# Modulation vectors added up on VectorE over two layers, and expert gathers planned with a longer landing

## The chip, the core and the metric

The kernel runs on one NeuronCore of a Trainium2 chip. Five engines with queues of their own work side by side: TensorE (matmuls and transposes; PE in the rows), VectorE (DVE), ScalarE (ACT), GpSimd (POOL) and SyncE (SP), which here issues the plain loads and stores. GpSimd issues the indirect ones. Each engine works through its queue strictly in order, and an instruction that waits holds up all behind it. The metric is device time in microseconds (us), the lower the better.

## The reference

Two blocks over 512 tokens of width 1024, in float32. The first block has two layers, each with three mixers: a gated delta rule, latent attention and a gated linear recurrence. The second block takes modulation vectors from two conditioning vectors `c` and `c_ctx`, runs differential attention and retention over 512 tokens and 256 context tokens, and then a mixture of 64 experts.

```python
mod_x = jax.nn.silu(c) @ ada_w[l] + ada_b[l]
mod_c = (jax.nn.silu(c_ctx) @ ada_w[l] + ada_b[l])[None]
...
sh1, sc1, g1, sh2, sc2, g2 = jnp.split(mod_x, 6, axis=-1)
csh1, csc1, cg1, csh2, csc2, cg2 = jnp.split(mod_c, 6, axis=-1)
...
x = x + g1[:, None] * y_x
h2 = modulate(rmsnorm_2(x, norm2_g), sh2, sc2)
ffn_x = moe_ffn(h2.reshape(b * s, d), router_w, router_bias, exp_w1, exp_w3, exp_w2,
                shared_w1, shared_w3, shared_w2).reshape(b, s, d)
x = x + g2[:, None] * ffn_x
...
def body(acc, inp):                       # in moe_ffn, over blocks of one expert's tokens
    tok, wt, e = inp
    xb = h_pad[tok]
    yb = (jax.nn.silu(xb @ w1[e]) * (xb @ w3[e])) @ w2[e]
    return acc.at[tok].add((yb * wt[:, None].astype(yb.dtype)).astype(acc.dtype)), None
```

`ada_w` is 1024 x 6144, and of `mod_c` only the first two of six parts are used. Each token goes to 8 of the 64 experts. The modulation vectors depend on the conditioning vectors alone, not on `x`, so they can be computed at any time before the second block.

## The kernel before

The kernel is written as a recording. Every engine call goes into a list (`Rec.add`), with its reads and writes, and at `flush` a list scheduler (`Rec.attempt`) replays the list on a model of the engines and so decides the order in which each engine's instructions are written. All instructions but a few thus have one source line (L411 before, L415 after). The model takes a duration from `cost` for each instruction, a latency from `lat` between dependent ones (2000 ns behind any DMA), and `move` (bytes over 360 per ns) for the transfer. A free engine takes the ready instruction with the highest priority, which is the longest path to the end plus a bias. An instruction with a `gate` is not ready before a given earlier instruction has started.

Tiles come from pools of fixed buffers. `s2`, `wh` and `wl` are 80 buffers of 128x512 (`b` in the rows); `wr` and `ad` are three and four of 128x1024 (`raw`). A matmul of full precision is done as three fp32r matmuls on a high and a low half of each operand; `split` makes the halves, the high one on ScalarE and the low one, a subtraction, on VectorE (`b<-raw,b`). Every weight goes through this, so each engine stands in the path of TensorE's weights.

The first block's layers run as merged generators: `merge` draws from the delta rule, the dense projections and, as a side stream, from `ada`, each in proportion to a weight. `ada` loads the modulation weights in 48 chunks of 128x1024 (six parts of eight), multiplies each chunk by a column of the conditioning vectors on ScalarE (for two vectors in the parts 0 and 1, for one in the others, 64 products) and adds up the products on GpSimd. The delta rule ends its preparation by writing its triangular blocks out (`mdiag`) and reading their diagonals back, with which `gdn_solve` begins.

The routed experts run one after the other (`expert`, `block`), each with a fixed number of slots (`CAPS`, 32 to 192). A block compares slots with positions, selects with four small matmuls against `aux` which token sits in each slot, reduces that on VectorE to a row index `ix`, gathers these rows of `h2d` into X by an indirect DMA from GpSimd, transposes X on TensorE (eight 128xc transposes `ps<-const,raw`), and runs the expert: 4 fp32 and 12 fp32r matmuls, an activation, two transposes, 12 fp32r matmuls. The result Y is scattered with addition into `accd`. An unused slot has an index beyond the tokens: the gather leaves it out, and the scatter sends it to one of 128 spare rows behind the 512. The gather's chain can't start before the instruction that `hold` names, `XAHEAD` marks back, with three marks for each expert; weight loads have their own marks (`RAHEAD`, nine).

## Time and profile before

| quantity | value |
|---|---|
| runs, us | 2386.49, 2395.57, 2395.74 (median 2395.57) |
| profiled execution, us | 2396.73, its span 2395.0 |
| TensorE busy | 2187.3 us, 91% |
| VectorE, ScalarE, GpSimd busy | 1619.6, 1087.7 and 534.6 us |
| mean granted TensorE clock | 0.947 of full speed |
| HBM read and written | 358.44 and 41.63 MB |

The stages by time: first layer to about 605 us, second layer to 1120, second block's projections, attention, retention and routing to 1600, routed experts to 2370, final norm. A row of busy times by stage has the stage, its length, then busy us and instruction count of TensorE, its weight loads (PEld), VectorE, ScalarE and GpSimd, then the granted clock, the DMA engines' mean busy share and GB/s. A row of waits has who waited, for whom, us in total, times and the longest. A row of grouped instructions has engine, operation, written and read tiles with shapes and count, then busy us and mean ns of one, then the engine's idle us before them and what ended it. A row of a timeline has start, duration, engine, operation, and in brackets the idle time before it and its releaser. A row of the chain has start, length, and what was worked on.

### The profile page before, as it was taken

How to read it: one execution, taken by the hardware profiler on the slowest of the kernel's cores; microseconds unless marked ns; L12 is line 12 of the kernel's file. 1: busy time of each engine (PE TensorE's matmuls, PEld its weight loads, DVE VectorE, ACT ScalarE, POOL GpSimd, SP SyncE). 2: the span in 40 equal slices, each digit the busy share in tenths (PEclk: the TensorE clock that was granted, in tenths of full speed). 3: DMA queues.
4: the chain of work that ended last, by engine and by line, in shares of the span. 5: the costliest groups of instructions: out<-in, count | busy, mean ns of one | idle time of the engine just before them, and what ended most of it. 6: DMA issues, size and time to landing. Idle time of an engine off the chain costs nothing.

```text
span 2395.0 us, 32613 instructions
## 1 busy us (share of the span) xinstructions
PE 2187.3 (91%) x10382; PEld 1546.5 (65%) x10382; DVE 1619.6 (68%) x3578; ACT 1087.7 (45%) x2272; POOL 534.6 (22%) x393
## 2 busy tenths in 40 slices
PE   6898988999999999999998879879998999999995
PEld 4677866677788877777886657656555555444442
DVE  7995577775695557767733675657676667776775
ACT  5555456453452365445432353335444444544443
POOL 3364334200021010001000132033232233222222
PEclk9998999899999999999998979989999999999998
DMA  5334354223222232314211025349999899999994
GB/s 191 119 102 127 118 172 146 86 84 124 94 78 74 78 116 75 92 63 143 71 54 53 23 66 198 132 116 348 288 341 282 267 294 313 340 334 302 307 311 130
DMA packets 191185, 398.13 MB, mean 166 GB/s; under 512 B 32169, under 2 KB 48297, under 8 KB 191010
## 3 DMA queue, kind: packets, MB, share of 16 engines
q1 hardware_dynamic: 178050, 356.24, 44.1%
q0 software_dynamic: 12960, 39.79, 7.6%
q8 instruction: 82, 1.34, 0.2%
q14 instruction: 93, 0.76, 0.1%
HBM read 358.44 MB, written 41.63 MB: 167 GB/s over the span
## 4 chain that ended last, share of the span: by engine, by line
PE 69%; DVE 13%; DMA 11%; ACT 3%; issue 3%; POOL 1%; SPq 0%; POOLq 0%; DVEq 0%; ACTq 0%
PE ps L411 69%; DVE b L411 10%; DMA raw<-h2d,m 5%; DVE m L411 3%; ACT b L411 3%; DMA accd<-raw,m 1%; DMA raw<-in_adaw_dram 1%; DMA raw<-in_wo_dram 1%; DMA b<-in_ew_dram 1%; POOL raw L411 1%; DMA xdiag<-b 0%; DMA raw<-in_wi_dram 0%; SPq L411 0%; DMA raw<-accd 0%; DMA b<-in_x_dram 0%
## 5 line engine op out<-in xcount | busy, mean ns | idle before, releaser
L411 PE MATMUL ps<-b,b 128*128 128x512 f32 (+9 forms) x8052 | 1870.1, 389 | 83.2 <-DVE b L411 49.6
L411 PEld LDWEIGHTS ps<-b,b 128*128 128x128 f32 (+6 forms) x8052 | 1312.6, 184 | 571.9 <-issue 130.1
L411 ACT ACTIVATE b<-ps 128x512 f32<-128x512 f32 (+16 forms) x661 | 271.1, 431 | 676.6 <-PE ps L411 599.6
L411 DVE TENSOR_TENSOR b<-b,b 128x512 fp32r<-128x512 f32 (+5 forms) x751 | 469.8, 664 | 35.2 <-ACT b L411 18.3
L411 ACT ACTIVATE b<-b 128x512 fp32r<-128x512 f32 (+3 forms) x702 | 393.8, 619 | 121.6 <-DVE b L411 84.5
L411 DVE TENSOR_TENSOR b<-raw,b 128x512 fp32r<-128x512 f32 (+2 forms) x340 | 240.0, 720 | 187.2 <-ACT b L411 173.7
L411 ACT ACTIVATE b<-raw 128x512 fp32r<-128x512 f32 (+3 forms) x348 | 207.2, 611 | 350.3 <-PE ps L411 256.0
L411 POOL DMA_INDIRECT accd<-raw,m x72 | 133.2, 1850 | 367.6 <-DVE raw L411 224.3
L411 PE MATMUL ps<-const,b 128*128 128x128 f32 (+5 forms) x898 | 159.5, 292 | 52.1 <-DVE b L411 39.0
L411 PEld LDWEIGHTS ps<-const,b 128*128 128x128 f32 (+5 forms) x898 | 115.0, 153 | 102.0 <-DVE b L411 49.4
L411 POOL TENSOR_TENSOR raw<-raw,raw 128x1024 f32<-128x1024 f32 x56 | 140.2, 2512 | 159.9 <-ACT raw L411 132.3
L411 PE MATMUL ps<-raw,b 128*96 128x512 f32 (+5 forms) x272 | 151.8, 676 | 5.3 <-ACT raw L411 2.9
L411 POOL DMA_INDIRECT raw<-h2d,m x68 | 100.9, 1483 | 231.0 <-PE ps L411 83.7
L411 DVE SCALAR_TENSOR_TENSOR raw<-ps,m,b 96x512 f32<-96x512 f32 (+5 forms) x136 | 97.5, 740 | 50.9 <-DMA accd<-raw,m 30.1
L411 DVE SCALAR_TENSOR_TENSOR b<-b,ps 128x512 f32<-128x512 f32 (+6 forms) x106 | 54.1, 510 | 102.7 <-ACT b L411 99.2
L411 POOL TENSOR_TENSOR m<-m,mhalf 128x1 f32<-128x1 f32 (+2 forms) x54 | 52.2, 968 | 301.6 <-DVE m L411 301.6
L411 DVE TENSOR_REDUCE m<-ps 128x1 f32<-128x256 f32 (+9 forms) x196 | 75.1, 393 | 60.5 <-PE ps L411 59.0
L411 DVE TENSOR_TENSOR b<-b,ps 128x512 f32<-128x512 f32 (+6 forms) x150 | 82.6, 559 | 49.2 <-PE ps L411 48.5
L411 DVE TENSOR_TENSOR b<-ps,b 128x512 fp32r<-128x512 f32 (+8 forms) x136 | 74.0, 545 | 47.1 <-ACT b L411 38.9
L411 POOL MEMSET b<- 64x512 f32 (+4 forms) x19 | 8.4, 454 | 398.1 <-PE ps L411 326.6
L411 DVE SCALAR_TENSOR_TENSOR b<-ps,cols,b 128x511 f32<-128x511 f32 (+3 forms) x118 | 86.9, 742 | 7.8 <-ACT b L411 6.9
L411 PE MATMUL ps<-const,raw 96*128 96x96 f32 (+5 forms) x544 | 61.0, 249 | 33.4 <-DMA raw<-h2d,m 30.4
(139 smaller groups left out, 1199.0 us busy)
## 6 DMA issues: line engine op xcount, KB each, us to landing
b<-in_ew_dram SPq DMA_DIRECT2D x640, 256.0 KB
raw<-in_wi_dram SPq DMA_DIRECT2D x100, 512.0 KB
raw<-in_ew_dram SPq DMA_DIRECT2D x64, 512.0 KB
raw<-in_adaw_dram SPq DMA_DIRECT2D x48, 512.0 KB
raw<-in_wo_dram SPq DMA_DIRECT2D x40, 512.0 KB
raw<-in_wuq_dram SPq DMA_DIRECT2D x24, 192.0 KB
b<-in_x_dram SPq DMA_DIRECT2D x16, 256.0 KB
zd<-b SPq DMA_DIRECT2D x16, 256.0 KB
```

The costliest lines, as they stand in the source:

```text
L411: getattr(getattr(nc, o.eng), o.fn)(*[real(x) for x in o.a], **{m: real(x) for m, x in o.k.items()})
```

## The change

In `ada` a chunk's product and addition become one VectorE instruction (`scalar_tensor_tensor`: chunk times column plus sum); only the first product of each sum stays on ScalarE. The side stream is drawn in four slices of 14 steps, one in each half of both layers, at low weights, and a gate keeps each of its instructions from being planned earlier than 60 recorded instructions before it. In the planner an indirect DMA costs 1500 instead of 900 ns of issue, and a gather lands 7000 instead of 2000 ns after its transfer; fp32r matmuls cost 11 ns more and fp32 ones up to 24. The gather's chain may begin nine marks back, three experts, instead of six. A scatter uses the gather's index and leaves out unused slots; the spare rows, their zeros and the second index go.

```diff
+from itertools import islice
...
 RW = 1497.6
 STEP = 4800.0
 AHEAD = 3
-XAHEAD = 6
+XAHEAD = 9
 XBIAS = 6900.0
 NATIVE = 4
-SIDE = ((160, 351), (130, 122))
+SIDE = (11, 12.5)
+SIDEN = 14
 NSLOT = 80
 NADA = 4
 TAGS = {"wl": 5, "wh": 5, "s2": None}
 NRAW = 7
 ADAPS = "tr"
 ADABIAS = 1000000.0
+ADALEAD = 60
 TAIL = 200
+DLAT = (2000.0, 7000.0)
 WIDE = (4, 6)
 LAST = 1
 LASTW = True
...
         if m == "call":
             return 500
         if "dma" in m:
-            return 60 if eng == "sync" else 900
+            return 60 if eng == "sync" else 1500
         n = size(outs[0])
         sb = all("PSUM" not in str(x.space) for x in outs + ins)
         if eng == "tensor":
...
             if dt == BF16:
                 return max(w, 54)
             if dt == F32R:
-                return w + 3 if size(ins[1]) >= 256 else max(4 * w, 108)
-            return max(4 * w, 216)
+                return w + 14 if size(ins[1]) >= 256 else max(4 * w, 108)
+            return max(4 * w + 24, 224)
         if eng == "scalar":
             return 70 + 0.87 * n + (200 if len(outs) > 1 else 50 if len(ins) > 1 else 0)
         if eng == "vector":
...
                 hold.setdefault(o.after, []).append(i)
 
         def lat(p, q):
-            return 2000.0 if "dma" in p.fn else LAT.get(p.eng + q.eng, TAIL)
+            return DLAT[p.k.get("in_offset") is not None] if "dma" in p.fn else LAT.get(p.eng + q.eng, TAIL)
 
         top = {}
         for o in reversed(ops):
...
                     self.issue = max(self.issue, t) + 480
                 self.dmaq = max(self.dmaq, t if e != "sync" else self.issue - 480) + o.move
                 end = self.dmaq
-            done = end + (2000 if "dma" in o.fn else TAIL)
+            done = end + (DLAT[o.k.get("in_offset") is not None] if "dma" in o.fn else TAIL)
             for nm in o.names[1]:
                 self.wrote[nm] = done
             for nm in o.uses:
...
         self.pairs, self.mixB = {}, []
         dense = chain(self.lru(l), self.mla_lat(l), self.mz(l))
         parts = [(self.gdn_chain(l), GW[l]), (dense, 100)]
-        run(merge(*parts, *([(side, SIDE[l][0])] if side else [])))
+        run(merge(*parts, *([(islice(side, SIDEN), SIDE[0])] if side else [])))
         self.load_x()
         self.rope_tables(self.A["const"], 256)
         src = lambda nh, k: self.A["wo"][l, nh, k]
...
                 if h == 3:
                     self.part = list(self.mixB)
 
-        run(merge((heads(), 100), (dense, 60), *([(side, SIDE[l][1])] if side else [])))
+        run(merge((heads(), 100), (dense, 60), *([(islice(side, SIDEN), SIDE[1])] if side else [])))
         run(self.out_proj(src, 4, self.part))
         run(self.out_proj(src, 8, self.mixB[4:8], last=True))
         self.dump_x(f"x{l}")
...
         g = iter(g)
         while True:
             self.nc.bias += ADABIAS
+            self.nc.gate = max(len(self.nc.ops) - ADALEAD, 0)
             try:
                 w = next(g)
             except StopIteration:
                 return
             finally:
                 self.nc.bias -= ADABIAS
+                self.nc.gate = None
             yield w
 
     def ada(self):
...
                     f = sc[:, 8 * v + k:8 * v + k + 1]
                     if not k:
                         nc.scalar.activation(acc[v], w, AF.Copy, scale=f)
-                        continue
-                    pr = w if v == nv - 1 else self.t2(tag="ad")
-                    nc.scalar.activation(pr, w, AF.Copy, scale=f)
-                    nc.gpsimd.tensor_tensor(out=acc[v], in0=acc[v], in1=pr, op=OP.add)
+                    else:
+                        nc.vector.scalar_tensor_tensor(acc[v], w, f, acc[v], op0=OP.mult, op1=OP.add)
                 yield 1.0
             if part < 2:
                 for v in range(nv):
...
 class K3(K2):
     def h2(self):
         nc = self.nc
-        self.acc = self.dr.tile([640, D], F32, name="accd")
+        self.acc = self.dr.tile([T, D], F32, name="accd")
         self.h2d = self.dr.tile([T, D], F32, name="h2d")
         G = [self.mrow(4, i) for i in range(2)]
         S = [self.mrow(3, i) for i in range(2)]
...
                 nr = self.t2()[:, :256]
                 nc.vector.tensor_tensor(out=s3(nr), in0=s3(rem), in1=d, op=OP.subtract)
                 rem = nr
-        self.dump_row = C(1, "dumprow")
-        nc.vector.tensor_scalar(self.dump_row, ipart, 512.0, None, op0=OP.add)
         pc = self.psum("a")
         for t in range(4):
             nc.tensor.matmul(pc[0:64, 0:1], mb[:, 64 * t:64 * t + 64], onesb[:, 0:1], start=(t == 0), stop=(t == 3))
...
         at4 = self.small(4, "at4", I32)
         for t in range(NT):
             nc.vector.tensor_scalar(at4[:, t:t + 1], self.c2[:, 385:386], 128.0 * t, None, op0=OP.add)
-        z = self.t2()
-        nc.gpsimd.memset(z, 0.0)
-        for i in range(2):
-            nc.sync.dma_start(self.acc[512:640, i * 512:(i + 1) * 512], z)
         ph = {(i, j): self.psum("mm") for i in range(2) for j in range(2)}
         at = []
         for h in range(2):
...
             nc.tensor.matmul(pm, oh[:, t, :], aux(t), start=(t == 0), stop=(t == 3))
         m = self.small(2, "m")[:c]
         nc.vector.tensor_reduce(m, pm.rearrange("p (a b) -> p a b", a=2), axis=AX.X, op=OP.add)
-        ix = self.small(2, "ix", I32)[:c]
-        nc.vector.tensor_scalar(ix[:, 0:1], m[:, 0:1], HUGE, None, op0=OP.add)
-        nc.vector.tensor_scalar(ix[:, 1:2], m[:, 0:1], HUGE, self.dump_row[:c], op0=OP.add, op1=OP.min)
+        ix = self.small(1, "ix", I32)[:c]
+        nc.vector.tensor_scalar(ix, m[:, 0:1], HUGE, None, op0=OP.add)
         xs = []
         X = self.t2(tag="wr")[:c]
-        nc.gpsimd.indirect_dma_start(out=X, out_offset=None, in_=self.h2d[:], in_offset=Ind(ix[:, 0:1]),
+        nc.gpsimd.indirect_dma_start(out=X, out_offset=None, in_=self.h2d[:], in_offset=Ind(ix),
                                      bounds_check=T - 1, oob_is_err=False)
         for h in range(2):
             px = self.psum("a")[:, :4 * c]
...
         Y = self.t2(tag=YTAG)[:c]
         for n in range(2):
             nc.vector.scalar_tensor_tensor(Y[:, 512 * n:512 * n + 512], ys[n], m[:, 1:2], self.g2[n][:c], op0=OP.mult, op1=OP.mult)
-        nc.gpsimd.indirect_dma_start(out=self.acc[:], out_offset=Ind(ix[:, 1:2]), in_=Y, in_offset=None, compute_op=OP.add)
+        nc.gpsimd.indirect_dma_start(out=self.acc[:], out_offset=Ind(ix), in_=Y, in_offset=None,
+                                     bounds_check=T - 1, oob_is_err=False, compute_op=OP.add)
 
     def hold(self, q):
         self.nc.gate = self.seen.get(q, self.mark)
```

On TensorE in the expert stage, from one expert's last slot-selection matmul (`aux`) to the transposes of that expert's X (`const,raw` with 128x48), before:

```order
L411 MATMUL ps_70<-aux,b_19467 48x6
L411 MATMUL ps_69<-const_152,b_19542 128x48 x2
L411 MATMUL ps_65<-raw_148,b_19555 48x512 x2
L411 MATMUL ps_65<-b_19203,b_19555 48x512
...
L411 MATMUL ps_67<-b_19538,b_19570 48x512
L411 MATMUL ps_67<-b_19589,b_19570 48x512
L411 MATMUL ps_67<-b_19538,b_19576 48x512
L411 MATMUL ps_71<-const_152,raw_150 128x48 x4
L411 MATMUL ps_72<-const_152,raw_150 128x48 x4
```

and now, at the same place (here the transposes of `raw_150` are those of the expert before, and those of `raw_151` this one's):

```order
L415 MATMUL ps_70<-aux,b_19447 48x6
L415 MATMUL ps_66<-raw_147,b_19559 48x512 x2
...
L415 MATMUL ps_66<-b_19546,b_19566 48x512
L415 MATMUL ps_71<-const_152,raw_150 128x48 x4
L415 MATMUL ps_72<-const_152,raw_150 128x48 x4
...
L415 MATMUL ps_70<-aux,b_19573 48x6
L415 MATMUL ps_65<-raw_146,b_19685 48x512 x2
...
L415 MATMUL ps_65<-b_19672,b_19692 48x512
L415 MATMUL ps_71<-const_152,raw_151 128x48 x4
L415 MATMUL ps_72<-const_152,raw_151 128x48 x4
```

One expert's matmuls stood between selection and transposes; now there are two experts' and one more set of transposes and selections. This holds for 47 of the 68 blocks; for the first few, the last ten and some between the distance is less.

On VectorE in the first layer behind the triangular solve (`b<-ps,m` scales an attention output, `m` are columns, `b<-raw,b` is a weight split), before:

```order
L411 SCALAR_TENSOR_TENSOR b_2336<-b_2327,ps_68 128x512
L411 TENSOR_REDUCE m_10_86<-b_2333 128x4
L411 TENSOR_TENSOR m_10_86<-m_10_86,m_37_113 128x4 x2
L411 TENSOR_SCALAR m_18_94<-m_10_86 128x4
L411 TENSOR_TENSOR b_2363<-raw_151,b_2356 128x512
```

and now:

```order
L415 TENSOR_TENSOR m_26_102<-m_26_102,m_54_130 128x4
L415 SCALAR_TENSOR_TENSOR b_1825<-b_2542,b_1825 128x512
L415 SCALAR_TENSOR_TENSOR raw_147<-raw_145,m_30_106,raw_147 128x1024
L415 SCALAR_TENSOR_TENSOR raw_148<-raw_145,m_30_106,raw_148 128x1024
L415 TENSOR_SCALAR m_3_79<-m_26_102 128x4
L415 TENSOR_TENSOR b_2575<-raw_150,b_2552 128x512
```

The two 128x1024 instructions on `raw` are the new multiply-adds of one chunk for both vectors; the weight split stands behind them. The first pair stands at instruction 362 of VectorE, 36 of the 56 before instruction 820, and the last 20 between 1160 and 1540, in the second layer. On SP's queue the loads of the input `x` are now first; before, two chunks of modulation weights were.

## Rows read from the trace of the kernel before

**Rows 1.** Busy time by stage, columns as above.
```profile
0.00:180.00 180.00, 142.32 (x649) 115.93 (x650) 154.75 (x360) 98.45 (x167) 83.61 (x67) 0.93 0.43 138
180.00:460.00 280.00, 253.88 (x1268) 199.58 (x1267) 180.44 (x308) 146.50 (x251) 103.10 (x49) 0.93 0.42 136
605.00:1120.00 515.00, 502.78 (x2562) 406.61 (x2560) 348.92 (x793) 242.50 (x506) 49.46 (x59) 0.99 0.29 90
1600.00:2340.00 740.00, 696.82 (x2960) 366.30 (x2959) 524.90 (x1130) 345.56 (x747) 220.57 (x132) 0.96 0.97 308
```

**Rows 2.** Waits of TensorE, whole span: us in total, times, longest.
```profile
PE ps L411 <- DVE b L411: 90.0, 63, 10.4
...
PE ps L411 <- DMA raw<-h2d,m: 30.4, 15, 4.7
```

**Rows 3.** Instruction groups of 128x1024 and 1x1024: busy us, mean ns.
```profile
L411 ACT ACTIVATE raw<-raw,m 128x1024 f32<-128x1024 f32 x64 | 73.1, 1144 | 17.1 <-DMA raw<-in_adaw_dram 12.1 <-PE ps L411 4.6 <-DMA modr<-raw 0.3
L411 POOL TENSOR_TENSOR raw<-raw,raw 128x1024 f32<-128x1024 f32 x56 | 140.2, 2512 | 159.9 <-ACT raw L411 132.3 <-DVE b L411 17.3 <-PE ps L411 6.9
L411 DVE SCALAR_TENSOR_TENSOR raw<-raw,raw 1x1024 f32<-1x1024 f32 x1 | 1.2, 1204 | 0.0
```

**Rows 4.** VectorE's groups, 0 to 180 us.
```profile
L411 DVE TENSOR_TENSOR b<-raw,b 128x512 fp32r<-128x512 f32 x39 | 31.5, 817 | 6.0 <-ACT b L411 5.9
...
L411 DVE TENSOR_TENSOR m<-m,m 128x16 f32<-128x16 f32 x11 | 7.7, 697 | 0.2
```

**Rows 5.** VectorE's groups, 180 to 460 us.
```profile
L411 DVE TENSOR_TENSOR b<-raw,b 128x512 fp32r<-128x512 f32 x43 | 38.3, 904 | 32.9 <-ACT b L411 32.9
L411 DVE SCALAR_TENSOR_TENSOR b<-b,b 128x512 f32<-128x512 f32 x16 | 18.9, 1182 | 2.1 <-POOL b L411 1.4 <-ACT b L411 0.5
```

**Rows 6.** VectorE's groups, 605 to 1120 us.
```profile
L411 DVE TENSOR_TENSOR b<-raw,b 128x512 fp32r<-128x512 f32 x112 | 76.1, 694 | 53.9 <-ACT b L411 51.5 <-PE ps L411 2.0
L411 DVE SCALAR_TENSOR_TENSOR b<-b,b 128x512 f32<-128x512 f32 x28 | 19.2, 687 | 8.4 <-ACT b L411 7.4 <-POOL b L411 0.7
...
L411 DVE TENSOR_TENSOR m<-m,m 128x16 f32<-128x16 f32 x11 | 1.8, 167 | 0.0
```

**Rows 7.** The chain that ended last, its start: start us, us, work.
```profile
1.23 4.82 DMA raw<-in_adaw_dram
...
15.01 0.88 DVE b L411 x2
```

**Rows 8.** SP's timeline: the diagonals read, and the second layer's start.
```profile
171.16 0.38 SPq L411 DMA_DIRECT2D b<-mdiag  x1
...
599.71 11.21 SPq L411 DMA_DIRECT2D xd<-b  x5
...
724.69 0.38 SPq L411 DMA_DIRECT2D b<-mdiag  x1
```

**Rows 9.** Waits of ScalarE, 0 to 610 us.
```profile
ACT raw L411 <- DMA raw<-in_adaw_dram: 12.1, 8, 3.1
```

**Rows 10.** TensorE's timeline: a selection and its transposes; two following groups of transposes.
```profile
2064.61 0.29 PE L411 MATMUL ps<-aux,b 128*64 128x6 bf16 x4
...
2079.99 0.71 PE L411 MATMUL ps<-const,raw 64*128 64x64 f32 x8 [1.10 <-DMA raw<-h2d,m]
...
2203.03 0.69 PE L411 MATMUL ps<-const,raw 48*128 48x48 f32 x8
...
2213.34 0.69 PE L411 MATMUL ps<-const,raw 48*128 48x48 f32 x8
```

**Rows 11.** TensorE's waits for gathers: the first, and one near the end.
```profile
1617.97 1.34 PE L411 MATMUL ps<-const,raw 96*128 96x96 f32 x8 [3.53 <-DMA raw<-h2d,m]
...
2312.69 0.43 PE L411 MATMUL ps<-const,raw 32*128 32x32 f32 x4 [1.37 <-DMA raw<-h2d,m]
```

**Rows 12.** Busy time of two stretches of 20 us.
```profile
1680.00:1700.00 20.00, 20.00 (x78) 12.04 (x77) 15.89 (x31) 9.77 (x20) 5.20 (x4) 1.00 1.05 344
...
1800.00:1820.00 20.00, 15.31 (x63) 8.57 (x62) 11.39 (x26) 7.26 (x16) 5.17 (x4) 0.83 0.76 206
```

## The prediction

> **What bounds the kernel now.** I read the busy time by stage first [rows 1]. Two regimes show. From 1600 to 2340 us, the routed experts, TensorE is busy 697 of 740 us and the DMA engines 97%: both are nearly full. From 605 to 1120 us, the second layer of the first block, TensorE is busy 503 of 515 us at a granted clock of 0.99, so TensorE alone bounds it. The first layer does the same work from 0 to 605 us and needs 90 us more: TensorE is idle 38 us of its first 180 and 26 us of the next 280, at a granted clock of 0.93 in both.
>
> Then I read whom TensorE waits for. VectorE is the largest item; in the expert stage the gathers (15 waits, 30.4 us) are the only large one, and expert weights are not in the list at all [rows 2]. So the change can gain in two places: the first layer, and the gather waits with the clock that they cost.
>
> **Modulation vectors.** Before, each of 64 products is a ScalarE pass of 1144 ns, and 56 of them are added on GpSimd at 2512 ns, 140 us in all, within the first layer [rows 3]. After, 8 ScalarE passes stay, the 56 adds go, and VectorE gets 56 fused multiply-adds of 128x1024. The trace has one VectorE instruction of this form, on one partition: 1204 ns [rows 3]. I take that for each: 56 x 1.204 = 67 us of new VectorE work. ScalarE loses 56 x 1.144 = 64 us, GpSimd 140 us.
>
> VectorE also wins something. The same forms are slower while GpSimd adds than in the second layer, where it doesn't [rows 4 to 6]. First 180 us: weight subtractions 39 x (817-694) ns = 4.8 us, 128x16 products 11 x (697-167) = 5.8 us, together 11 us. From 180 to 460 us: 43 x (904-694) = 9.0 us and 16 x (1182-687) = 7.9 us, together 17 us. These are the largest groups only, so the excess is not less than 28 us.
>
> A rule bears on this. The Trainium skill, SBUF — State Buffer, section "SBUF: two separate sides", says that a VectorE instruction with two SBUF inputs and a GpSimd instruction take a port pair as an exclusive lock, the later one waiting out the other. Taken literally an add could hold VectorE for its whole 2.5 us, 140 us in all; the rows of the largest groups show 28 us, and the sum uses the rows. The rule also speaks against the change, since each new multiply-add would hold off GpSimd for 1.2 us, 67 us in all; no row has TensorE waiting for GpSimd.
>
> *Start.* The first two chunks of the modulation weights stand ahead of the input rows on SP's queue and lead the chain for 4.8 us [rows 7]. After, the input rows are first: -4 us (bounds -4.8 and 0).
>
> *Up to the triangular solve.* In the new VectorE order 362 instructions precede the first multiply-add; before, VectorE runs 360 in the first 180 us [rows 1]. So this stage becomes free of modulation work. From its first VectorE work (15.0 us) to the read of the block diagonals (171.2 us) it takes 156 us; the same piece of the second layer, from 599.7 to 724.7 us, takes 125 us [rows 7, 8]. The difference, 31 us, is the most to gain; the largest VectorE groups account for 11. The passes that ScalarE loses and the clock come on top, so I take two thirds of the ceiling: -21 us (bounds -31 and 0).
>
> *Rest of the first layer.* 36 of the 56 multiply-adds now stand here, 43 us of VectorE against at least 17 us of lost excess: 26 us more on an engine with 100 us idle in 280 [rows 1]. That idle time hides it; if the cover fails it costs 26 us, and if TensorE's idle 26 us came back, it would gain those. Between them, with the freed ScalarE: -4 us.
>
> *Second layer.* The other 20, 24 us, go where VectorE is busy 349 of 515 us. Bounds 0 and +24; TensorE is the bound there, so +4 us.
>
> What is queued behind a multiply-add: it waits for its 512 KB chunk, and behind it on VectorE stand the weight splits that TensorE needs. Before, ScalarE stood in this place and waited 12.1 us, in 8 of the 48 chunks [rows 9]. This lies inside the bounds above, and has a rival below.
>
> Layers together: -4 - 21 - 4 + 4 = -25 us.
>
> **Gathers: planned later, issued earlier.** At full clock one expert takes 10.31 us of TensorE, the distance between two groups of input transposes [rows 10]. Before, from an expert's slot-selection matmuls to its transposes there is one period less these two (0.69 and 0.29 us): 9.3 us. In the new order a whole expert more stands between: 19.6 us. Selection, GpSimd's issue and landing have to fit in. A long one: selection at 2064.61, transposes released at 2079.99, so 15.4 us [rows 10]. That overruns 9.3 and fits 19.6. For the first four, the last ten and some seven between, the distance stays near the old one.
>
> So of the 30.4 us the first wait (3.53 us) and those of the last ten experts (1.37 us and a smaller one) stay; 25 us go [rows 2, 11], where one of the seven can still wait. The bounds are 0 and -27.
>
> Stalls also cost clock: in a full stretch it is 1.00, in one with a stall and 15.31 of 20 us busy it is 0.83 [rows 12], a mixture of the 1.2 and 2.4 GHz levels. In the whole stage 0.04 x 740 = 30 us of full-speed work is missing; two thirds of it, -20 us, I put to the waits that go (bounds 0 and -27).
>
> Late next are the weights. The stage moves 740 us x 308 GB/s = 228 MB; at the 344 GB/s of the full stretch [rows 12] that is 663 us, under the some 700 us that would remain. So DMA keeps a cover of about 5%, less than before: +3 us for new waits (bounds 0 and +30, had DMA to stay near its present rate). Padded scatter rows: the capacities add up to 5104 slots for at most 4096 tokens, so some 1000 rows of 4 KB go, 4 MB written and as much read for the accumulation, 12 to 24 us of DMA time by the same rate. TensorE doesn't wait for it, so I count nothing, but it widens the cover. One small VectorE instruction less per block, a zero tile and two stores less: nothing, for VectorE is idle 215 us of this stage.
>
> X lives longer in its buffer, some 20 us of a turn of 31 us with three buffers, so GpSimd gets no new wait there, and the scatters behind it none.
>
> Experts: -25 - 20 + 3 = -42 us.
>
> **New TensorE costs in the planner** (11 ns more for each fp32r matmul, 24 for fp32 ones) reorder everything, the attention stage of the second block too. No row tells the sign: 0, with the spread of the three runs (2386.5 to 2395.7) as bounds, -9 and +9.
>
> **Sum.** -25 - 42 = -67 us. The profiled run took 2396.7 us (span 2395.0, and 1.7 around it), 1.1 us over the median of 2395.6: 2396.7 - 67 - 1.1 = 2328.6, 2328 us. What a measurement here can tell from no change is about 0.5%, 12 us.
>
> **Rivals.**
> 1. *The multiply-adds become TensorE's wait in both layers.* For: TensorE already waits longest for VectorE [rows 2], and in the new order up to ten multiply-adds stand within 28 instructions. Against: 100 and 166 us of VectorE idle in these stages. Price, nothing hidden: -4 - 21 + 26 + 24 = +25, with the experts' -42: -17, 2379 us. Chance 0.13.
> 2. *Weights bound the experts.* For: DMA at 97% [rows 1]. Against: 228 MB fit in 663 us, and TensorE's waits don't name weights. With the +30 in full the experts give -15: -25 - 15 = -40, 2356 us. A milder form is gathers that still land late because the queues are fuller. Chance 0.11.
> 3. *Slower: VectorE stands still for each chunk.* The planner's landing for plain loads is unchanged, 2 us after the transfer, while a chunk leads the chain for 4.8 us at the start [rows 7]; in parts 0 and 1 each chunk goes to the same buffer, so none is loaded ahead. If each of 48 chunks holds VectorE and with it TensorE for 3.1 us, the longest wait of ScalarE before [rows 9], that is +149: with -25 and -42, +82, 2478 us. It decides from 67/48 = 1.4 us for every chunk; before it was 12.1/48 = 0.25 us. Chance 0.07.
>
> The forecast itself has 0.69, with a range of its own from 2290 to 2362: half of both gains gives 2362; the gather and clock bounds (12 more), the ceiling before the solve (10) and three quarters of the idle time behind it (16) give 2290. The whole range adds the reordering on the low side and reaches rival 1 on the high side: 2284 to 2380. It leaves out rival 3 and the tails. Faster by over 0.5% (under 2384 us): the forecast, rival 2 and most of rival 1, 0.88. Within: 0.05. Slower: rival 3, 0.07.
>
> **What would show it.** Right: TensorE's waits for gathers fall from 30 us to under 8 and stay only in the first and last experts; granted clock of the expert stage 0.98 or more, in some 700 us with DMA at 95% or above; weight subtractions near 694 ns in the first 180 us; the diagonals read near 146 us; multiply-adds near 1.2 us, with VectorE waiting for modulation chunks by less than 20 us. Wrong: TensorE waiting for weight splits in the second layer, VectorE waiting for chunks by over 1.4 us each, or an expert stage of 740 us with weights among the waits.

## The result, and the profile after

The changed kernel takes 2356.48 us (median; 2348.46 to 2360.68) where the kernel before took 2393.39 in the same comparison: a ratio of 0.985 (95% interval 0.982 to 0.988). That is faster, by 37 us. The forecast was 67 us. The time lies inside the stated range, and inside the forecast's own range (2290 to 2362), near its far end. The profiled execution took 2356.11 us, its span 2354.2.

The stages, from the profiled executions. They are cut at SP's instructions that begin the second layer and the second block, at the first matmul of the routed experts and at TensorE's last. Kernels that are alike up to a cut differ there by 2 to 4 us.

| stage, us | before | after | difference | forecast |
|---|---|---|---|---|
| first layer | 599.7 | 554.8 | -44.9 | -29 |
| second layer | 506.1 | 533.5 | +27.4 | +4 |
| second block up to the routed experts | 490.3 | 486.6 | -3.7 | 0 |
| routed experts | 775.9 | 757.4 | -18.5 | -42 |
| final norm | 23.0 | 21.9 | -1.1 | 0 |

The busy time by stage of the changed kernel, cut for its own stages (columns as in [rows 1], which it answers):

```profile
0.00:135.00 135.00, 120.55 (x596) 99.37 (x597) 111.81 (x358) 73.58 (x145) 30.60 (x47) 1.00 0.43 136
...
555.00:1090.00 535.00, 514.92 (x2546) 407.52 (x2545) 369.83 (x800) 238.76 (x494) 48.94 (x55) 0.97 0.34 108
1578.00:2300.00 722.00, 693.31 (x2964) 361.31 (x2963) 515.73 (x1064) 343.19 (x747) 247.10 (x132) 0.98 0.97 309
```

The start runs at the full granted clock, the second layer below its old 0.99, and the experts at 0.98 instead of 0.96.

Waits of the changed kernel over the whole span (who waits, for whom, us in total, times, longest), against [rows 2]:

```profile
DVE raw L415 <- DMA accd<-raw,m: 71.0, 25, 9.2
PE ps L415 <- DVE b L415: 65.1, 56, 6.1
...
PE ps L415 <- DMA const<-in_const_dram: 12.9, 1, 12.9
```

None of TensorE's rows names a gather any more. The first row has grown: VectorE waits for scatters (`accd<-raw,m`) before it may write the next Y into their buffer. It has 25 waits of up to 9.2 us, 71.0 us in the expert stage; in the kernel before there were 13:

```profile
DVE raw L411 <- DMA accd<-raw,m: 30.1, 13, 5.3
```

In the expert stage alone (1575 to 2333 us) TensorE waits for VectorE by 26 us, where the kernel before had 6.9 us:

```profile
PE ps L415 <- DVE b L415: 17.2, 8, 4.6
PE ps L415 <- DVE m L415: 8.5, 6, 4.2
```

Groups of instructions of the changed kernel (columns as in [rows 3]):

```profile
L415 POOL DMA_INDIRECT accd<-raw,m x72 | 184.9, 2568 | 356.0 <-DVE raw L415 315.2 <-DVE b L415 29.3 <-DVEq L2274 8.1
L415 DVE SCALAR_TENSOR_TENSOR raw<-ps,m,b 96x512 f32<-96x512 f32 (+5 forms) x136 | 98.4, 741 | 93.1 <-DMA accd<-raw,m 71.0 <-PE ps L415 20.7
...
L415 DVE SCALAR_TENSOR_TENSOR raw<-raw,m,raw 128x1024 f32<-128x1024 f32 x56 | 72.4, 1313 | 5.1 <-DMA raw<-in_adaw_dram 2.9 <-ACT raw L415 2.2
```

The last row is the new multiply-add: 1313 ns, and 2.9 us of waiting for chunks in all. The second is Y's writing, which pays for the scatters.

VectorE's groups in the first 135 us, against [rows 4]:

```profile
L415 DVE TENSOR_TENSOR b<-raw,b 128x512 fp32r<-128x512 f32 x38 | 26.3, 699 | 5.7 <-ACT b L415 4.0 <-PE ps L415 1.5
L415 DVE TENSOR_TENSOR m<-m,m 128x16 f32<-128x16 f32 x11 | 1.8, 166 | 0.0
```

The same forms took 817 and 697 ns beside GpSimd's additions.

SP's timeline, against [rows 8]: the diagonals read in the first layer, the second layer's start, the diagonals in the second layer.

```profile
124.58 0.36 SPq L415 DMA_DIRECT2D b<-mdiag  x1
...
554.78 3.05 SPq L415 DMA_DIRECT2D xd<-b  x2
...
677.73 0.36 SPq L415 DMA_DIRECT2D b<-mdiag  x1
```

All of the first layer's gain stands ahead of the triangular solve (171.16 to 124.58); from there to the second layer it is 430.2 us after and 428.6 before.

How a wait for a scatter reaches TensorE (timeline of all engines; start, duration, and in brackets the idle time before and its releaser):

```profile
1924.58 2.56 POOL L415 DMA_INDIRECT accd<-raw,m  x1 [8.21 <-DVE b L415]
...
1934.95 1.40 DVE L415 SCALAR_TENSOR_TENSOR raw<-ps,m,b 64x512 f32<-64x512 f32 x2 [9.24 <-DMA accd<-raw,m]
...
1938.80 0.36 PE L415 MATMUL ps<-const,b 80*128 80x80 f32 x2 [3.90 <-DVE b L415]
```

GpSimd issues a scatter at 1924.58. VectorE, which has the next expert's Y to write, stands still for 9.24 us until it has landed at 1934.95. Behind it in the queue stands the next expert's activation, and TensorE waits 3.90 us for it under the name `DVE b`. So the scatter is named in VectorE's waits, while TensorE's waits name VectorE.

### The profile page after: what moved, and what is told of

Same layout as the page of the kernel before. It is cut to its first block, busy times and chain, and to the rows that moved or that the text cites. A ratio compares the mean times of both kernels' runs of the same rounds, so it can differ in the third digit from the quotient of the medians.

```text
span 2354.2 us, 32673 instructions
## 1 busy us (share of the span) xinstructions
PE 2185.0 (93%) x10382; PEld 1533.8 (65%) x10382; DVE 1604.6 (68%) x3565; ACT 1028.7 (44%) x2216; POOL 422.3 (18%) x336
## 5 line engine op out<-in xcount | busy, mean ns | idle before, releaser
L415 PE MATMUL ps<-b,b 128*128 128x512 f32 (+10 forms) x8052 | 1883.6, 391 | 70.3 <-DVE b L415 33.8
L415 DVE TENSOR_TENSOR b<-b,b 128x512 fp32r<-128x512 f32 (+5 forms) x751 | 456.7, 646 | 36.1 <-ACT b L415 18.6
L415 DVE TENSOR_TENSOR b<-raw,b 128x512 fp32r<-128x512 f32 (+2 forms) x340 | 227.3, 680 | 186.2 <-ACT b L415 175.4
L415 POOL DMA_INDIRECT accd<-raw,m x72 | 184.9, 2568 | 356.0 <-DVE raw L415 315.2
L415 PE MATMUL ps<-raw,b 128*96 128x512 f32 (+5 forms) x272 | 140.6, 620 | 4.1 <-DMA raw<-in_ew_dram 1.7
L415 POOL DMA_INDIRECT raw<-h2d,m x68 | 73.5, 1081 | 198.6 <-PE ps L415 86.2
L415 DVE COPY b<-ps 128x128 f32<-128x128 f32 (+2 forms) x134 | 50.3, 381 | 58.4 <-PE ps L415 48.0
L415 POOL TENSOR_TENSOR b<-b,b 128x128 f32<-128x128 f32 (+1 forms) x62 | 45.9, 768 | 213.3 <-DVE b L415 138.5
```

Source lines behind the costliest of these rows:

```text
L415: getattr(getattr(nc, o.eng), o.fn)(*[real(x) for x in o.a], **{m: real(x) for m, x in o.k.items()})
```

## The experiments

All medians are beside the kernel before on the same chip; it was at 2388 to 2395 us there.

**One part at a time.** *The modulation part alone*, in the kernel before:

```diff
-SIDE = ((160, 351), (130, 122))
+SIDE = (11, 12.5)
+SIDEN = 14
...
-                    pr = w if v == nv - 1 else self.t2(tag="ad")
-                    nc.scalar.activation(pr, w, AF.Copy, scale=f)
-                    nc.gpsimd.tensor_tensor(out=acc[v], in0=acc[v], in1=pr, op=OP.add)
+                        nc.vector.scalar_tensor_tensor(acc[v], w, f, acc[v], op0=OP.mult, op1=OP.add)
```

> The kernel before with the modulation part of the change alone (multiply-adds on VectorE, slices of 14 steps, the gate). Theory: the first layer's gain and the second layer's loss both come from this part. Second layer's first store of x about 45 us earlier than before (554.8 against 599.7), the second block's start 18 us earlier, the experts as before with some 30 us of gather waits: about 2375 us, ratio 0.992. Rival: the start and the second layer's 27 us come from the new TensorE costs in the planner; then the second layer stays near 506 us here and the total is about 2348, ratio 0.981.

Measured: 2361.93 us, ratio 0.985 (0.982 to 0.987). First layer 549.6 us (-50), second 520.5 (+14), experts 779.2 with the old waits for gathers:

```profile
PE ps L414 <- DMA raw<-h2d,m: 34.3, 16, 5.1
```

So this part alone has the ratio of the whole change. The second layer lies between the two expectations (533 and 506 us), and so does the time (2375 and 2348).

*The gather planning alone*, in the kernel before:

```diff
-XAHEAD = 6
+XAHEAD = 9
+DLAT = (2000.0, 7000.0)
...
-            return 60 if eng == "sync" else 900
+            return 60 if eng == "sync" else 1500
```

> The kernel before with the gather part alone: issue 1500 ns, landing 7000 ns, nine marks; padded scatter rows stay. Theory (scatter landing): gather waits of TensorE vanish, but VectorE's waits for a scatter's landing before it writes the next Y rise from 30 to about 60 us because the planner still lands a scatter after 2 us; expert stage 18 us shorter, ratio 0.992, GpSimd's scatter issue stays at 1.85 us. Rival (bounded scatter): the rise from 30 to 65 us and the longer issue (1.85 to 2.57 us) come from the scatter that leaves out slots; then VectorE's wait stays near 30 us here and the experts gain 30 to 40 us, ratio 0.984 to 0.987.

Measured: 2399.26 us, ratio 1.003 (1.000 to 1.005). Experts 770.4 us (-5). In that stage:

```profile
DVE raw L412 <- DMA accd<-raw,m: 54.4, 21, 6.2
...
PE ps L412 <- DVE raw L412: 18.8, 8, 5.9
...
PE ps L412 <- DMA raw<-h2d,m: 3.4, 2, 2.2
```

The waits for gathers go from 30.4 to 3.4 us. VectorE's waits for scatters rise from 30 to 54 us, and TensorE gets 18.8 us of waiting for Y's writing (`DVE raw`). One wait took the place of the other, as the theory has it; but the stage gained 5 us where it expected 18, and the whole gained nothing.

*The modulation part and the gather planning together*, with old matmul costs and padded rows (both edits above):

> The kernel before with the modulation part and the gather planning alone (padded scatter rows and old matmul costs stay). The gather planning alone gained 5 us in the expert stage (776 to 770 us), yet the kernel without matmul costs has 755 us there. Theory: it is the order that decides, not the padded rows: 752 to 762 us in the experts, 2336 to 2346 us in all. Rival: the padded rows cost the difference: 768 to 775 us, 2352 to 2362 us in all.

Measured: 2351.73 us, ratio 0.983 (0.979 to 0.986), between the two expectations; experts 768.2 us, as the rival has it. Inconclusive on the padded rows, since the ratio's interval overlaps that of the kernel without the new matmul costs, further below.

**The scatter's rows.** *The changed kernel with the padded rows put back* (the second index and the 128 spare rows):

```diff
-        nc.gpsimd.indirect_dma_start(out=self.acc[:], out_offset=Ind(ix), in_=Y, in_offset=None,
-                                     bounds_check=T - 1, oob_is_err=False, compute_op=OP.add)
+        nc.gpsimd.indirect_dma_start(out=self.acc[:], out_offset=Ind(ix[:, 1:2]), in_=Y, in_offset=None, compute_op=OP.add)
```

> The changed kernel with the padded scatter rows put back. Theory (scatter landing): same time as the changed kernel within 0.4%, VectorE's wait for scatters stays at 50 us or more. Rival (bounded scatter): scatter issue falls back to 1.85 us, VectorE's wait for scatters to about 30 us, and the kernel is 10 to 20 us faster than the changed one, ratio 0.977 to 0.981.

Measured: 2352.9 us, ratio 0.982 (0.980 to 0.985); experts 756.9 us, VectorE's waits for scatters 69.8 us. No difference from the changed kernel: leaving the rows out neither gains nor causes the waits. Nor does it make the issue longer, as the rival had it: a scatter's issue takes 2585 ns here, and 2413 in the gather planning alone, which has the padded rows too (1850 before, 2568 in the change).

**What VectorE waits for.** *The planner told that scatters land late too*:

```diff
-            return DLAT[p.k.get("in_offset") is not None] if "dma" in p.fn else ...
+            return DLAT["indirect" in p.fn] if "dma" in p.fn else ...
```

> The changed kernel with the planner's landing of 7000 ns for scatters too. Theory (scatter landing): the planner keeps Y's buffer closed until the scatter has landed, VectorE's wait for scatters falls from 65 us to under 25, TensorE's waits for VectorE in the expert stage from 26 to under 10, and the experts gain another 10 to 15 us: about 2343 us, ratio 0.979. Rival: with four buffers shared by Y and weight loads the wait only moves to SyncE's queue or the weights; no gain, ratio 0.985.

Measured: 2385.6 us, ratio 0.995 (0.994 to 0.997), a miss. The waits for scatters fall to 35.5 us, but the experts take 782.6 us, with TensorE waiting 22.5 us for Y's writing and again for gathers. In the order, Y and the weights now take turns in all four buffers. A landing nearer to the measured one (in this run 7.9 us from issue to landing, median) made the time longer, not shorter; why this order is worse was not followed further.

*The same program with scatters that write instead of adding*; every engine has the same instructions in the same order, and the experts' sums are left out:

```diff
-                                     bounds_check=T - 1, oob_is_err=False, compute_op=OP.add)
+                                     bounds_check=T - 1, oob_is_err=False)
```

> The changed kernel with its 68 scatters writing instead of adding (the sums of the experts are left out); every engine has the same instructions in the same order. Theory: after the change TensorE's gather waits are gone because VectorE's waits took their place; it may not write the next Y before the scatter that last used the buffer has landed, and the landing is long because each row is read, added and written. Then VectorE's waits for scatters fall from 71 us in the expert stage to under 40, and the time falls by 6 to 20 us. Rival: the landing is long because of GpSimd's issue (2.6 us mean) and the full queues, not because of the addition: waits stay at 55 to 75 us and the time within 4 us of the changed kernel. Second rival: the waits fall but TensorE has cover for them; waits under 40, time within 4 us.

Measured: 2337.99 us, ratio 0.978 (0.975 to 0.980), 18 us under the changed kernel, as the theory expects. Experts 734.8 us, 22.6 less, while the stages before them stay within 3 us. Waits in the expert stage and busy time of 1600 to 2300 us:

```profile
DVE raw L415 <- DMA accd<-raw,m: 26.1, 11, 7.3
```

```profile
1600.00:2300.00 700.00, 686.83 (x2991) 354.19 (x2990) 518.16 (x1066) 341.61 (x746) 209.04 (x128) 1.00 0.92 312
```

Waits down from 71 to 26 us, clock 1.00, and 734.8 us is what the forecast hoped for (775.9 - 42 = 734). The addition thus accounts for 45 us of VectorE's waits and for 22.6 us of the stage. It also lengthens the issue on GpSimd, which falls from 2568 to 2119 ns without it. A scatter that only writes still makes VectorE wait 26 us. The same weights come in, in less time and at a lower DMA share.

*Five buffers instead of four in the pool `ad`*:

```diff
-NSLOT = 80
-NADA = 4
+NSLOT = 78
+NADA = 5
...
-NRAW = 7
+NRAW = 8
```

> The changed kernel with five buffers of 128x1024 in place of four in the pool that holds Y and the modulation chunks (two fewer of 128x512). Theory (VectorE waits for Y's buffer until its scatter has landed): VectorE's waits for scatters fall from 71 us to under 30, the expert stage from 757 us to 740 to 750, the whole by 6 to 18 us. Rival (the buffer is not what binds, the planner only finds another order with other waits): waits of TensorE in the expert stage stay near 30 us and the time within 5 us of the changed kernel.

Measured: 2357.04 us, ratio 0.985 (0.982 to 0.987); waits for scatters 65.2 us. Waits and total failed the theory; the experts' 749.8 us just meet it, but the first layer is 7 us longer (561.8). The reason for the waits stands in the order: the planner gives the same buffer to many experts in a row. In the changed kernel 18 scatters in a row read `raw0` (and later 23), while the weight loads take turns in the other three (buffers of the scatters in GpSimd's order, and of a stretch of the weight loads in SP's):

```
raw0 raw0 raw0 raw0 raw0 raw0 raw0 raw0 raw0 raw0 raw0 raw0 raw0 raw0 raw0 raw0 raw0 raw0
raw2 raw1 raw3 raw2 raw1 raw3 raw2 raw1 raw3 raw2 raw1 raw3
```

One of each expert's weight tiles has the size 128x1024, is loaded up to three experts ahead (nine marks), and lives in the same pool as Y. With five buffers the planner still gives Y the same one for up to nine experts in a row, until about 2035 us; from there on Y goes through all five in turn. All 65.2 us of waits lie ahead of that point and none behind it (61.9 and 9.1 us in the changed kernel).

*Five buffers, of which two are for Y alone* (and, in the layers, for the modulation sums); the lines of the five buffers are as above:

```diff
...
-YTAG = "ad"
+YTAG = "y"
...
-        self.nc.pool("ad", self.rw[:NADA])
+        self.nc.pool("ad", self.rw[:3])
+        self.nc.pool("y", self.rw[3:NADA])
...
-            acc = [self.t2(tag="ad") for _ in range(nv)]
+            acc = [self.t2(tag="y") for _ in range(nv)]
```

> The changed kernel with one buffer of 128x1024 more (two fewer of 128x512, as with five buffers) and the five buffers split: three for weights and modulation chunks, two that only Y (and before it the modulation sums) may take. In the changed kernel and with five buffers in one pool the planner gives one and the same buffer to up to 18 experts in a row, since weights loaded three experts ahead hold the others; with two of its own Y alternates, and a scatter has one expert more (10 us) to land. Theory (Y's single buffer makes VectorE wait for the scatter): VectorE's waits for scatters fall from 71 us to under 15, the expert stage from 757 us to 733 to 745, the whole by 10 to 24 us. Rival (waits for scatters are long because the DMA queues are full at a share of 0.98, whichever buffer is taken): waits stay above 40 us, the time within 6 us of the changed kernel.

Measured: 2338.23 us, ratio 0.977 (0.974 to 0.980); five buffers in one pool gave 0.985. Experts 742.7 us. Waits of that stage, and busy time of 1600 to 2300 us:

```profile
DVE raw L415 <- DMA accd<-raw,m: 8.8, 1, 8.8
```

```profile
1600.00:2300.00 700.00, 683.80 (x2967) 353.77 (x2966) 518.87 (x1060) 340.42 (x744) 235.67 (x127) 0.99 0.97 312
```

25 waits become one, with the DMA share still at 0.97. So neither full queues nor the number of buffers in the pool decide on these waits, but whether Y has the next buffer free. Part of the wait moves on: GpSimd now waits 35.4 us, in 7 waits, for an earlier scatter before it issues the next. Of the stage's gain of 14.7 us, 7.6 had come with the fifth buffer already. The difference of the totals is not the experts' alone: the second layer takes 522.9 instead of 533.5 us, and the first 561.9 instead of 554.8. The final norm takes 28.5 instead of 21.9 us, which the last experiment below explains.

**The second layer.** *All modulation steps in the first layer*:

```diff
-SIDE = (11, 12.5)
-SIDEN = 14
+SIDE = (22, 25)
+SIDEN = 28
```

> The changed kernel with all 56 steps of the side stream drawn in the first layer (two slices of 28 at twice the weight), none in the second. Theory: what the second layer lost (506 to 533 us) is the price of the 20 multiply-adds, of the 12 moved column sums on TensorE (7 us) and of the waits and lower clock that they cause; so it returns to 506 to 512 us, and the first layer goes from 555 to 570 to 585 us; total within 6 us. Rival: the second layer lost by the planner's new matmul costs: it stays at 525 to 535 us, and the total is 10 to 25 us slower.

Measured: 2359.48 us, ratio 0.985 (0.982 to 0.988). The first layer (571.9 us) and the total are as the theory expects; the second layer takes 522.3 us, between the two expectations, so neither was right alone. *The changed kernel without the new matmul costs*:

```diff
-                return w + 14 if size(ins[1]) >= 256 else max(4 * w, 108)
-            return max(4 * w + 24, 224)
+                return w + 3 if size(ins[1]) >= 256 else max(4 * w, 108)
+            return max(4 * w, 216)
```

> The changed kernel with the planner's old costs for matmuls. The modulation part alone had a second layer of 520 us where the changed kernel has 533. Theory: the new matmul costs reorder that layer at a loss; without them it takes 518 to 524 us and the whole is 6 to 14 us faster. Rival: an order of the planner is better in one stage and worse in another by chance; the second layer differs, but the total stays within 5 us of the changed kernel.

Measured: 2340.35 us, ratio 0.978 (0.976 to 0.981), 16 us under the changed kernel, as the theory expects; first layer 547.1 us, second 520.2. The second layer of four kernels, from one profile each:

| second layer, us | old matmul costs | new matmul costs |
|---|---|---|
| without multiply-adds | 506.1 (before) | 522.3 (all in the first layer) |
| with 20 multiply-adds | 520.2 | 533.5 (the change) |

Each of the two costs 11 to 16 us whether the other is there or not. Busy time of the second layer with multiply-adds and the old costs, then with the new costs (each its own kernel):

```profile
547.00:1067.00 520.00, 502.19 (x2541) 402.59 (x2540) 368.43 (x797) 237.69 (x488) 46.64 (x55) 0.99 0.35 110
```

```profile
555.00:1088.00 533.00, 512.92 (x2537) 405.87 (x2536) 367.97 (x796) 236.90 (x489) 48.94 (x55) 0.97 0.34 107
...
855.00:875.00 20.00, 13.36 (x45) 7.72 (x44) 14.88 (x18) 14.46 (x29) 5.17 (x3) 0.83 0.54 187
```

As many instructions on every engine, 2 us more idle time, but 11 us more TensorE time at a lower clock. In the slice of 20 us the new order has TensorE busy for 13.36 us, and the clock is 0.83. Cut into slices of 20 us, the layer has five with a clock of 0.92 or less in the new order (0.74 the lowest) and two in the old (0.83 and 0.85). Summed over the slices, the clock takes some 15 us from the new order and some 7 from the old, an estimate that covers most of the 11 us.

**The parts that help, together.** *No new matmul costs, and Y with two buffers of its own*, by the two edits shown above:

```diff
-                return w + 14 if size(ins[1]) >= 256 else max(4 * w, 108)
+                return w + 3 if size(ins[1]) >= 256 else max(4 * w, 108)
...
-YTAG = "ad"
+YTAG = "y"
```

> The changed kernel without the planner's new matmul costs (which alone was 16 us faster than it) and with Y's two buffers of its own. If both effects add up: 2314 to 2332 us, layers as without the costs (second block from 1067 us), experts in 733 to 745 us. Rival: the order found without the new costs already had cover (its waits for scatters are 54 us): experts stay at 750 to 757 us and the time at 2335 to 2345 us.

Measured: 2320.34 us, ratio 0.971 (0.968 to 0.974), as the sum of both expects. Experts 736.2 us; the granted clock of its span is 0.958. VectorE's waits for scatters in that stage are 12.8 us, and GpSimd's are 59.4. SP's timeline at its end:

```profile
2295.25 1.29 SPq L415 DMA_DIRECT2D raw<-accd  x3
2302.90 3.80 SPq L415 DMA_DIRECT2D out_dram<-raw  x3
2306.75 0.44 SPq L415 DMA_DIRECT2D raw<-accd  x1
2314.79 0.33 SPq L415 DMA_DIRECT2D out_dram<-raw  x1
```

The final norm takes four tiles from a pool that now has three buffers, so the fourth is read 11.5 us after the first. *The fourth tile from Y's pool*:

```diff
-            at = self.t2(tag="ad")
+            at = self.t2(tag="ad" if t < 3 else "y")
```

> The version with Y's own buffers and without the new matmul costs, with the fourth tile of the final norm in one of Y's buffers. With three buffers for weights that tile was read back 11 us after the other three and its norm ended last (28.6 us from TensorE's end to the span's end, against 22.0 with four buffers). Nothing ahead of the final norm is moved. Theory: the end comes 4 to 7 us earlier, 2313 to 2317 us. Rival: the write of the outputs ends last anyway: within 2 us of 2320.

```profile
2291.98 1.76 SPq L415 DMA_DIRECT2D raw<-accd  x4
2299.16 6.36 SPq L415 DMA_DIRECT2D out_dram<-raw  x4
```

Measured: 2318.19 us, ratio 0.970 (0.967 to 0.972). The end behind TensorE's last matmul goes from 28.6 back to 22.2 us in the profile; the median lies between the two expectations and cannot be told from the version above, whose interval overlaps. It is the fastest measured, some 37 us under the changed kernel by the ratios, whose intervals are well apart (that of the changed kernel is 0.982 to 0.988).

## Why the prediction was right or wrong

Direction and range were right, the size was not: -37 us by the medians against -67. Three terms of the sum failed, in both directions.

*Experts: "+3 us for new waits", put to the weights.* This is the term that failed most. The waits for gathers went, and further than forecast (30.4 us to none, even in the first and last experts, where some were expected to stay). The clock rose from 0.96 to 0.98, by which some 15 of the forecast's 20 us of full-speed work came back (0.02 of 757 us, an estimate). But the forecast asked which wait would be next only of the weights and of X's buffer, and said that "the scatters behind it" get no new wait. It did not follow Y's buffer, although VectorE already waited 30 us for scatters before. With gathers late, little of that wait reached TensorE (6.9 us for VectorE in the stage); without them it grew to 71 us, and 26 us reached TensorE (17.2 and 8.5 us under `DVE b` and `DVE m`). So TensorE's idle time in the stage fell by 14 us only (44 to 31) and its busy time by 5 (731.7 to 726.4). Without the addition it is idle for 18.6 us and busy for 716.4, which is 26 and 15 us less than before. Three runs show that Y's buffer held the gain back: without the addition the stage takes 734.8 us, with two buffers for Y alone 742.7, and with old matmul costs and those two buffers 736.2, which is -39.6 for the forecast's -42. So the gain was about rightly sized, and the wait for Y's buffer withheld over half of it.

*New TensorE costs in the planner: "0", bounds -9 and +9.* They cost 16 us, above the bound. The spread of runs of one order says nothing on the spread between orders. The first layer lost 8 us, the second 13, and the second block up to the experts gained 7.

*Layers: -25 us.* With the old costs it is -39, with the new -18, so two errors cancelled in part. Up to the triangular solve -25 was forecast with the start, and -46.6 came. The ceiling of 31 us was not one. It took the second layer's piece of 125 us as the shortest, but the first layer's now takes 112 us from TensorE's first matmul (12.9 us) to the read: the new order puts less work ahead of the diagonals (550 matmuls in the first 125 us, where before 610 stood in 171). The causes named were there: the subtractions went from 817 to 699 ns, the clock from 0.93 to 1.00, and TensorE's 38 us of waits for VectorE in that stretch to about 1 us. No run parts them. The start itself gave nothing: TensorE's first matmul is at 12.9 us instead of 10.4, because the identity now lands behind the input rows. *Rest of the first layer*: -4 forecast, +2 came, -6 in the modulation part alone. *Second layer*: "+4 us" where the trace says +14 for the modulation part, 6 of it the twelve column sums that TensorE took along (`ps<-raw,ones`, 5.8 us busy in that layer, none there before), which no term had. The bound of +24 held for the multiply-adds, but not for the +27 with the new costs.

*Right, or nearly:* the multiply-add (1204 ns forecast, 1313 measured, 72 us in all for 67), waits for chunks under 20 us (2.9), padded rows at nothing. One sum does not come out: 2290 and the bound of -9 for the reordering give 2281, not 2284, for the low end of the range; nothing hangs on it.

*The rule on the port pair that the prediction cites:* the sum went by the rows, and the rows answer it: without GpSimd's additions the subtractions are back at 699 ns. That GpSimd is held off by the multiply-adds cannot be seen on TensorE.

*The rivals.* Rival 1 (multiply-adds bind in both layers) fell in the first layer and was half right in the second, +14 of its +24. Rival 2 named 2356 us, the very time measured, and was still wrong in its cause: TensorE waits 1.7 us for expert weights, and the same loads fit into 734.8 us. Rival 3 fell: 2.9 us of waits for 48 chunks.

*Left open:* what in the planner's order with the new matmul costs makes both layers worse (in the second, most of it shows as clock), why the order with late scatters is slower, why TensorE's busy time in the expert stage fell less than the clock rose, and whether the padded rows cost anything in the order with the old costs (768 against 755 us of experts, but ratios that overlap).

## What to carry to other kernels

When a wait that ends last is taken away, list for the same stretch what every engine waits for, not only the bounding one, and follow each buffer of the chain from its last reader to its next writer; the wait that comes up next may be in the trace already, as here, on an engine that TensorE hardly waits for yet. In a pool that a prefetch and a result share, the prefetch can take all buffers but one: give the result two of its own before adding buffers to the pool. New costs in a planner, even if meant to be nearer to the truth, need not give a faster order: measure such an edit alone.

## What the runs showed of the hardware

A scatter is slow to release its source: from the start of an adding scatter's issue at 1924.58 us to VectorE's next write into the buffer at 1934.95 it took 10.4 us, the length of a whole expert. Its issue on GpSimd took 2568 ns on average in the changed kernel and 1865 in that with the old matmul costs, where the same 72 scatters stand in another order.

The same scatter in the program with addition and in that without: with it, from 1689.22 us to VectorE's write at 1701.17, 12.0 us; without it, from 1683.32 to 1693.54, 10.2 us. Writing instead of adding, with all else in place, brought the DMA share of the expert stage from 0.98 to 0.92 between 1600 and 2300 us at the same GB/s (311 and 312).

The Trainium skill, DMA: Bandwidth & Descriptors, section "Anatomy of one DMA — SWDGE (gpsimd) path", fits a DMA issued by GpSimd as 2.0 us and the bytes at 436 GB/s; for 128 rows of 4 KB, the most that such a scatter can write, that is an estimate of 3.2 us. The trace differs: for the scatter at 1924.58 us, from the end of its issue (1927.14) to VectorE's write, it took 7.8 us, and for the one that only writes, from 1687.13 to 1693.54, 6.4 us. So the addition is not all of the difference; what the busy queues give to it no run here shows.
